# Projection stores from GpSimd's queue instead of SyncE's, in a hybrid attention and mLSTM encoder layer

## The chip, the cores and the metric

The kernel runs on one core of one Trainium2 chip. The metric is the device time of one execution in microseconds (us). The core has five engines, each of which works through its own queue of instructions in order: TensorE (PE in the profile; its weight loads are PEld), VectorE (DVE), ScalarE (ACT), GpSimd (POOL) and SyncE (SP). DMA transfers are issued by SyncE and by GpSimd, and carried out by 16 DMA engines that both share. In the profile the transfers of SyncE are queue q1 (hardware_dynamic), those of GpSimd queue q0 (software_dynamic).

## What is computed

One encoder layer over two sequences, a prompt of 1024 tokens and a sample of 2048, each with 16 learned meta tokens ahead of it and a model width of 1024:

```python
xn = _rmsnorm(h, g_pre)
proj = xn @ w_in + b_in
na_q, na_k, na_v, na_z, ml_qk, ml_v, ml_z, ml_o, ml_g, mg = jnp.split(proj, SPLIT_IDX, axis=-1)
ya = _neighbourhood_attention(na_q, na_k, na_v, na_rpb)
ya = (ya * jax.nn.silu(na_z)) @ w_a
yb = (_mlstm_branch(ml_qk, ml_v, ml_g, ml_o, ml_conv_w, ml_head_g) * jax.nn.silu(ml_z)) @ w_b
ga, gb = jnp.split(jax.nn.sigmoid(mg), 2, axis=-1)
y = (ga * ya + gb * yb) @ w_out
return h + _rmsnorm(y, g_post)
```

The input projection has 6672 columns. Neighbourhood attention has 8 heads of width 64 on a grid of rows of 64 tokens, with windows of 8 by 16; the mLSTM has 4 heads of width 128 and runs in both directions. All products are taken in float32, which the kernel makes from a high and a low part: three matmuls for one.

## The kernel before

**Two strands.** `run` weaves two generators into one order of TensorE's instructions. `dense` does the projections and, at the end, the merge and output products; `sparse` does the token mixers, in the order of `STEPS`: mLSTM of the prompt, attention of the prompt, mLSTM of the sample, attention of the sample. Each strand yields after some matmuls with their estimated cost, and `run` lets the other go on by as much. A strand of `sparse` starts when the columns that it needs are done. `PLAN` names the order of `dense`: which 1024 tokens, and which columns (m and v for mLSTM and values, n for attention, g for the merge gates), and then six final blocks of 512 tokens.

**Order within the queues.** TensorE's order is the order in which the program was written. The queues of the other engines, SyncE's and GpSimd's too, are ordered when the kernel is built (`schedule_with_timeline_sim=True`), by when a model of the chip takes an instruction to be ready. Two helpers tie this order: `held()` queues VectorE's and ScalarE's instructions behind those traced so far, and `behind()` (L205) queues what is traced in it behind `self.marks`, the last instruction that `mark(start)` saw on VectorE, ScalarE and SyncE. `mark` is called after each projection evacuation (in `fm_evac` and `tm_unit`) and after each piece of `sparse`. The loads of `tload` (L944), the stores of normalised inputs in `beside` (L562) and the side work on weights and inputs are traced inside `behind()`.

**Feature-major columns.** `fm_half` takes 128 columns of the projection as weights (a tile `whl` with their high and low parts, four copies, loaded in `wpump`, L304 and L310) and 512 tokens as the moving side, 24 matmuls in `mm3` (L218 to L220) into a PSUM bank `pj` of three. `fm_evac` brings the result into an SBUF tile `st` (four copies) with bias, activation and scale; the columns z take a second copy of `st`. Then the tile is stored to a tensor in device memory: MQ and MK for the mLSTM (L714, and L716 for the meta tokens), GT, NQ, NK, NZ and SZ for the rest (L723), and a small padded copy of the meta tokens' keys, NKM (L730). `sgates`, which does the attention and gate columns with seven half products for eight, ends in the same `fm_evac`; its matmuls are L988 to L990.

**Token-major columns.** `tm_unit` takes tokens as weights and 256 or 264 columns as the moving side (L787 to L789), for the values (NV, MV), the output gate (TO) and the mLSTM's gates (GA). Two blocks of 128 tokens are gathered in a tile `stT` (four copies) and `tm_store` writes them: GA at L825 and L827, TO at L830, MV at L834 and L836, the meta tokens' values NVM at L840, and NV at L846, four transfers a tile.

**Who reads what is stored.** The mLSTM loads MK and MQ (`raw`, L1433), MV (`va`, L1503), SZ and TO (L1634, L1635), its own keys again (`kf`, L1616) and rows of decay (`um`, L1622). The attention loads NQ, NK, NKM, NV, NVM and NZ (L1184 to L1220). The final blocks load GT (`tg`, L1892).

**What GpSimd does.** It issues the stores of NV (L846), the loads and stores of the side work (`wprep`: `pr` L587 and `po` L605; `nprep`: `xr` L619, L634, L635; `tprep`: `xr` L664, L678), the attention's masks (`kx`, L1200) and one-hot rows (`qB`, L1113), and it clears small tiles. All other transfers are issued by SyncE, among them the loads of the weights (`whl`, `wraw` L289), the stores of prepared weights (L341), the inputs (`xr` L408, `xt` L415) and the outputs.

Of the kernel before, what the change touches and what calls it, by code (L numbers as in the profile page):

```python
# [18 lines left out]
P = 128  # L19
# [3 lines left out]
NM = 16  # L23
# [115 lines left out]
class K:  # L139
# [542 lines left out]
    def fm_evac(self, col, s, t0, meta, chunks, ps):  # L682

        nc, wp = self.nc, self.wp
        bi = (col // P) if col < 4608 else 36 + (col - 4624) // P
        bias = self.bfm[:, bi:bi + 1]
        start = len(nc.cur_bb.bb.instructions)
        st = wp.tile([P, HALF], F32, name="st", bufs=4)
        m = NM if meta else 0
        n = 512 + m  # L690
        for (c0, c1), p in zip(chunks, ps):
            o, q = st[:, c0:c1], p[:, :c1 - c0]
            if s == 0 and col < C_GA:
                b = max(c0, m)
                if b > c0:
                    nc.vector.tensor_tensor(q[:, :b - c0], q[:, :b - c0], self.rm, op=ALU.mult)
                nc.vector.tensor_tensor(q[:, b - c0:], q[:, b - c0:], self.rr[:, t0 // 512, b - m:c1 - m], op=ALU.mult)
            if col < C_NK:
                nc.scalar.activation(o.rearrange("p (b r c) -> p r b c", r=8, b=4), q.rearrange("p (r b c) -> p r b c", r=8, b=4),
                                     AF.Identity, bias=self.bq8[:, bi:bi + 1], scale=0.125)  # L700
            elif C_NZ <= col < C_MQ or C_MZ <= col < C_MO:
                zb = wp.tile([P, HALF], F32, name="st", bufs=4)
                nc.scalar.activation(zb[:, c0:c1], q, AF.Identity, bias=bias)
                nc.scalar.activation(o, q, AF.Tanh, bias=self.bfh[:, bi:bi + 1], scale=0.5)
                nc.vector.scalar_tensor_tensor(o, o, 1.0, zb[:, c0:c1], op0=ALU.add, op1=ALU.mult)
            elif col >= C_GA:
                nc.scalar.activation(o, q, AF.Tanh, bias=self.bfh[:, bi:bi + 1], scale=0.5)
            else:
                nc.scalar.activation(o, q, AF.Identity, bias=bias)
        if C_MQ <= col < C_MV:  # L710
            dst = (self.MQ if col < C_MK else self.MK)
            h = (col % 512) // P
            lo = 0 if meta else NM + t0
            nc.sync.dma_start(dst[s][h][:, lo:lo + n], st[:, :n])  # L714
            if meta:
                nc.sync.dma_start(dst[1 - s][h][:, :NM], st[:, :NM])  # L716
            self.mark(start)
            return
        if col >= C_GA:
            dst = self.GT[s][(col - C_GA) // P]  # L720
        else:
            dst = (self.NQ, self.NK, None, self.NZ, None, None, None, self.SZ)[col // 512][s][(col % 512) // P]
        nc.sync.dma_start(dst[:, t0:t0 + 512], st[:, m:n])  # L723
        self.mark(start)
        if meta and C_NK <= col < C_NV:
            km = wp.tile([P, 64], F32, name="km", bufs=1)
            nc.gpsimd.memset(km, 0.0)
            nc.gpsimd.tensor_copy(km[:, 8:24], st[:, :NM])
            nc.gpsimd.tensor_copy(km[:, 40:56], st[:, :NM])
            nc.sync.dma_start(self.NKM[(col % 512) // P][:, :], km)  # L730

    def fm_half(self, col, w, x, s, t0, meta, done=None, tags=None, late=None):
        if not meta:
# [77 lines left out]
    def tm_store(self, col, wd, s, n, cnt, tok, st):  # L811
        nc, wp = self.nc, self.wp

        def rows(d, c0, c1, lo):
            return d[lo:lo + n * cnt, c0:c1].rearrange("(a p) c -> p a c", p=n)

        f = col % 512
        if col >= C_MO:
            c0 = col - C_MO
            no = min(wd, 512 - c0)  # L820
            if wd > no:
                g = wd - no
                if tok is None:
                    for q in range(2):
                        nc.sync.dma_start(self.GA[q][0:NM, :], st[:n, 0, no:wd])  # L825
                else:
                    nc.sync.dma_start(rows(self.GA[s], 0, g, NM + tok), st[:, :, no:wd])  # L827
            if tok is not None:
                nc.scalar.activation(st[:, :, :no], st[:, :, :no], AF.Tanh, scale=0.5)
                nc.sync.dma_start(rows(self.TO[s], c0, c0 + no, tok), st[:, :, :no])  # L830
        elif col >= C_MV:
            if tok is None:
                for q in range(2):
                    nc.sync.dma_start(self.MV[q][0:NM, f:f + wd], st[:n, 0, :wd])  # L834
            else:
                nc.sync.dma_start(rows(self.MV[s], f, f + wd, NM + tok), st[:, :, :wd])  # L836
        else:
            if tok is None:
                for lo in (8, 40):
                    nc.sync.dma_start(self.NVM[lo:lo + NM, f:f + wd], st[:n, 0, :wd])  # L840
            else:
                for a in range(cnt):
                    for r in range(2):
                        row = (tok + a * P) // 64 + r
                        dst = self.NV[s][:, row * 8:row * 8 + 8, f:f + wd]
                        nc.gpsimd.dma_start(dst, st[r * 64:r * 64 + 64, a, :wd])  # L846
# [1356 lines left out]
```

## Time and profile before

| what | value |
|---|---|
| median of 3 runs | 2685.29 us (2685.11 to 2685.42) |
| the profiled execution | 2684.88 us |
| its span, first to last instruction | 2682.8 us |
| mean granted clock of TensorE over the span | 0.996 |
| HBM read, written | 543.72 MB, 253.60 MB |

The profile is of one execution. Its lines name an engine, a line of the kernel and an operation, with "out<-in" for the tiles that it writes and reads. A wait stands as "who <- what released it", with the total in us, the number of waits and the longest. "SPq" and "POOLq" are the queues in which SyncE and GpSimd issue DMA transfers. A stretch of time stands as from:to, its length, the busy time of each engine with its number of instructions, the granted clock of TensorE (PEclk, 1.00 is full speed), the mean busy share of the 16 DMA engines and the rate in GB/s. Matmuls overlap, so the busy time of TensorE counts overlapping ones once.

### The profile page before, as it was taken

The page shows a single profiled execution, that of the slowest core. Times are in us where ns is not written, and L with a number is a line of the kernel's source. Part 1 is how long each engine was busy: PE and PEld are TensorE (multiplying, and loading weights), DVE is VectorE, ACT ScalarE, POOL GpSimd, SP SyncE. Part 2 cuts the span into 40 slices and gives each one's busy share as a digit, 9 for nine tenths or more (in the row PEclk, how much of TensorE's full clock was granted, in tenths as well). Part 3 has the DMA queues.
Part 4 walks back from the last instruction along what each step waited for, and adds up shares of the span by engine and source line. Part 5 has one row for each costly group of instructions (what it writes and reads, how often), then busy time and mean ns, then how long its engine had stood idle before and what let it go on. Part 6 is the DMA issues. An engine that isn't in the chain of part 4 may idle for free.

```text
span 2682.8 us, 47074 instructions
## 1 busy us (share of the span) xinstructions
PE 2640.1 (98%) x15928; PEld 2330.7 (87%) x15928; DVE 1940.1 (72%) x5262; ACT 1441.0 (54%) x3388; POOL 195.3 (7%) x418
## 2 busy tenths in 40 slices
PE   9999998999999999999999999999999999999998
PEld 7998897899978999888888888887889898989888
DVE  5655678788667878546686776867478989898954
ACT  5423555554445655546665666656366666656521
POOL 0111130011301115000000000000000000000000
PEclk9999999999999999999999999999999999999999
DMA  9899988799866998978889998899899999998975
GB/s 370 331 334 335 331 289 306 278 339 312 294 223 235 328 331 289 319 234 285 261 270 346 362 299 261 273 351 336 281 312 319 288 306 287 280 304 261 310 255 209
DMA packets 393520, 800.49 MB, mean 298 GB/s; under 512 B 50528, under 2 KB 173360, under 8 KB 389440
## 3 DMA queue, kind: packets, MB, share of 16 engines
q1 hardware_dynamic: 361728, 697.24, 77.9%
q0 software_dynamic: 31552, 100.25, 10.1%
q8 instruction: 126, 2.06, 0.3%
q14 instruction: 114, 0.93, 0.1%
HBM read 543.72 MB, written 253.60 MB: 297 GB/s over the span
## 4 chain that ended last, share of the span: by engine, by line
PE 89%; DVE 4%; DMA 4%; ACT 1%; issue 1%; SPq 0%; POOL 0%; DVEq 0%; ACTq 0%
PE pj L218 9%; PE pj L220 9%; PE pj L219 9%; PE pj L988 8%; PE pj L990 7%; PE pj L989 7%; PE pj L787 5%; PE pj L789 5%; PE pj L788 5%; PE pj L1950 3%; PE pj L1949 3%; PE pj L1951 3%; PE sm L1283 3%; PE tr L1268 2%; DMA whl<-w 1%
## 5 line engine op out<-in xcount | busy, mean ns | idle before, releaser
L218 PE MATMUL pj<-xh,whl 128*128 128x512 f32 (+1 forms) x960 | 369.5, 385 | 8.2 <-DMA whl<-w 6.2
L220 PE MATMUL pj<-xh,whl 128*128 128x512 f32 (+1 forms) x960 | 361.3, 376 | 0.0
L219 PE MATMUL pj<-xl,whl 128*128 128x512 f32 (+1 forms) x960 | 360.4, 375 | 0.2 <-DVE xl L446 0.2
L787 PE MATMUL pj<-whl,xh 128*128 128x256 f32 (+1 forms) x1152 | 330.7, 287 | 0.0
L789 PE MATMUL pj<-whl,xl 128*128 128x256 f32 (+1 forms) x1152 | 327.0, 284 | 0.0
L788 PE MATMUL pj<-whl,xh 128*128 128x256 f32 (+1 forms) x1152 | 326.7, 284 | 0.0
L787 PEld LDWEIGHTS pj<-whl,xh 128*128 128x128 f32 x1152 | 219.0, 190 | 0.4
L1949 PE MATMUL pj<-whl,mh 128*128 128x256 f32 x768 | 218.3, 284 | 0.9 <-DMA whl<-w 0.9
L788 PEld LDWEIGHTS pj<-whl,xh 128*128 128x128 f32 x1152 | 218.9, 190 | 0.2
L789 PEld LDWEIGHTS pj<-whl,xl 128*128 128x128 f32 x1152 | 218.8, 190 | 0.0
L218 PEld LDWEIGHTS pj<-xh,whl 128*128 128x128 f32 x960 | 181.2, 189 | 40.8 <-issue 5.3
L1950 PE MATMUL pj<-whl,mh 128*128 128x256 f32 x768 | 216.3, 282 | 0.0
L1951 PE MATMUL pj<-whl,mlo 128*128 128x256 f32 x768 | 215.5, 281 | 0.0
L220 PEld LDWEIGHTS pj<-xh,whl 128*128 128x128 f32 x960 | 181.3, 189 | 35.0
L219 PEld LDWEIGHTS pj<-xl,whl 128*128 128x128 f32 x960 | 181.6, 189 | 30.4 <-issue 1.0
L988 PE MATMUL pj<-xh,whl 128*128 128x512 f32 x512 | 206.7, 404 | 1.1 <-ACT pj L1005 1.1
L990 PE MATMUL pj<-xh,whl 128*128 128x512 f32 x512 | 202.0, 395 | 0.0
L989 PE MATMUL pj<-xl,whl 128*128 128x512 f32 x512 | 201.0, 393 | 0.0
L1275 DVE TENSOR_TENSOR pts<-tr,pts 96x384 fp32r<-96x384 f32 (+2 forms) x192 | 118.6, 617 | 57.2 <-ACT pts L1270 55.2
L1270 ACT ACTIVATE pts<-tr 96x384 fp32r<-96x384 f32 (+2 forms) x192 | 103.6, 539 | 100.8 <-PE tr L1268 100.1
L218 PE MATMUL pj<-yh,whl 128*128 128x512 f32 x384 | 154.1, 401 | 0.0
L219 PE MATMUL pj<-yl,whl 128*128 128x512 f32 x384 | 151.5, 394 | 0.7 <-DVE yl L1851 0.7
(380 smaller groups left out, 6866.1 us busy)
## 6 DMA issues: line engine op xcount, KB each, us to landing
whl<-w SPq DMA_DIRECT2D x131, 1024.0 KB
whl<-q SPq DMA_DIRECT2D x112, 512.0 KB
w<-whl SPq DMA_DIRECT2D x36, 1024.0 KB
wraw<-wu SPq DMA_DIRECT2D x48, 512.0 KB
gt<-st SPq DMA_DIRECT2D x96, 256.0 KB
tg<-gt SPq DMA_DIRECT2D x96, 256.0 KB
q<-po POOLq DMA_DIRECT2D x26, 512.0 KB, 6.7
xt<-xt SPq DMA_DIRECT2D x24, 512.0 KB
```

The costliest lines, as they stand in the source:

```text
L218: mm(out, ah, bh, start=start, stop=False)
L219: mm(out, ah, bl, start=False, stop=False)
L220: mm(out, al, bh, start=False, stop=stop)
L787: nc.tensor.matmul(o, xh, wh, start=k == 0, stop=False)
L788: nc.tensor.matmul(o, xh, wl, start=False, stop=False)
L789: nc.tensor.matmul(o, xl, wh, start=False, stop=k == KT - 1)
L988: mm(bank, w[:, 0, k], xh[:, k], start=fresh and k == 0, stop=False, skip_group_check=True)
L989: mm(bank, w[:, 0, k], xl[:, k], start=False, stop=False, skip_group_check=True)
L990: mm(bank, w[:, 1, k], xh[:, k], start=False, stop=k == 3, skip_group_check=True)
L1949: nc.tensor.matmul(o, mh[:, k, xs], wh, start=clear > 0 and k == 0, stop=False)
L1950: nc.tensor.matmul(o, mh[:, k, xs], wl, start=False, stop=False)
L1951: nc.tensor.matmul(o, ml[:, k, xs], wh, start=False, stop=clear < 2 and k == KT - 1)
```

## The change

Ten lines in `fm_evac` and `tm_store` issue their transfer from GpSimd's queue instead of SyncE's. Tensors, tiles, shapes and the order of the matmuls are the same. The stores of NV were issued by GpSimd already.

```diff
@@ fm_evac
-            nc.sync.dma_start(dst[s][h][:, lo:lo + n], st[:, :n])
+            nc.gpsimd.dma_start(dst[s][h][:, lo:lo + n], st[:, :n])
             if meta:
-                nc.sync.dma_start(dst[1 - s][h][:, :NM], st[:, :NM])
+                nc.gpsimd.dma_start(dst[1 - s][h][:, :NM], st[:, :NM])
...
-        nc.sync.dma_start(dst[:, t0:t0 + 512], st[:, m:n])
+        nc.gpsimd.dma_start(dst[:, t0:t0 + 512], st[:, m:n])
...
-            nc.sync.dma_start(self.NKM[(col % 512) // P][:, :], km)
+            nc.gpsimd.dma_start(self.NKM[(col % 512) // P][:, :], km)
@@ tm_store
-                        nc.sync.dma_start(self.GA[q][0:NM, :], st[:n, 0, no:wd])
+                        nc.gpsimd.dma_start(self.GA[q][0:NM, :], st[:n, 0, no:wd])
                 else:
-                    nc.sync.dma_start(rows(self.GA[s], 0, g, NM + tok), st[:, :, no:wd])
+                    nc.gpsimd.dma_start(rows(self.GA[s], 0, g, NM + tok), st[:, :, no:wd])
             if tok is not None:
                 nc.scalar.activation(st[:, :, :no], st[:, :, :no], AF.Tanh, scale=0.5)
-                nc.sync.dma_start(rows(self.TO[s], c0, c0 + no, tok), st[:, :, :no])
+                nc.gpsimd.dma_start(rows(self.TO[s], c0, c0 + no, tok), st[:, :, :no])
         elif col >= C_MV:
             if tok is None:
                 for q in range(2):
-                    nc.sync.dma_start(self.MV[q][0:NM, f:f + wd], st[:n, 0, :wd])
+                    nc.gpsimd.dma_start(self.MV[q][0:NM, f:f + wd], st[:n, 0, :wd])
             else:
-                nc.sync.dma_start(rows(self.MV[s], f, f + wd, NM + tok), st[:, :, :wd])
+                nc.gpsimd.dma_start(rows(self.MV[s], f, f + wd, NM + tok), st[:, :, :wd])
         else:
             if tok is None:
                 for lo in (8, 40):
-                    nc.sync.dma_start(self.NVM[lo:lo + NM, f:f + wd], st[:n, 0, :wd])
+                    nc.gpsimd.dma_start(self.NVM[lo:lo + NM, f:f + wd], st[:n, 0, :wd])
```

## The prediction

> **What bounds the kernel now.** I read the first page first: busy times, queues, and the chain that ended last.
>
> ```profile
> span 2682.8 us, 47074 instructions
> ...
> PE 2640.1 (98%) x15928; PEld 2330.7 (87%) x15928; DVE 1940.1 (72%) x5262; ACT 1441.0 (54%) x3388; POOL 195.3 (7%) x418
> ...
> q1 hardware_dynamic: 361728, 697.24, 77.9%
> q0 software_dynamic: 31552, 100.25, 10.1%
> ...
> PE 89%; DVE 4%; DMA 4%; ACT 1%; issue 1%; SPq 0%; POOL 0%; DVEq 0%; ACTq 0%
> ```
>
> TensorE is busy for 2640.1 of 2682.8 us and the chain runs along it. Its 15928 matmuls stay as they are, so what can be won or lost is its idle time (42.7 us) and what its clock loses. Beside it the DMA engines are nearly full: q1 (what SyncE issues) and q0 (what GpSimd issues) take 88% of them. Next I asked for TensorE's waits over the whole run (waiter, releaser, total us, times, longest), then for the stretches just behind the long ones (from:to, length, PE busy, granted clock, DMA share, GB/s).
>
> ```profile
> PE sm L220 <- DVE ktl L1574: 7.0, 6, 2.6
> PE pj L218 <- DMA whl<-w: 6.2, 2, 3.9
> ...
> PE sc L1699 <- ACT kh L1661: 2.8, 1, 2.8
> PE sm L218 <- ACT kth L1573: 1.9, 1, 1.9
> ...
> PE sc L1700 <- DVE kl L1662: 0.4, 1, 0.4
> ```
>
> ```profile
> 692.00:699.00 7.00, 6.99 (x35) 0.56 1.00 378
> 793.00:798.00 5.00, 4.53 (x13) 0.66 1.03 409
> 1817.00:1822.00 5.00, 4.64 (x20) 0.66 0.81 260
> ```
>
> The waits are few and short, but three of them (1.9 us before 691, 3.9 us before 793, 2.8 us before 1816) are followed by a stretch at a granted clock of 0.56 or 0.66, which costs another 7.0 x 0.44 = 3.1, 5.0 x 0.34 = 1.7 and 1.7 us. In all three a load was late, two of them behind ScalarE, whose own waits name them.
>
> ```profile
> ACT v L1679 <- DMA va<-mv: 8.8, 5, 3.8
> ...
> ACT kh L1661 <- DMA kf<-kf: 7.0, 4, 2.3
> ```
>
> `va` was the one before 691, `whl` before 793, `kf` before 1816. Those loads stand in SyncE's queue, and so do the stores that the change moves.
>
> **Why a load is late.** The chain of waits around 447 us shows a queue that takes only so many transfers at once: the load of `whl` was issued the moment that `wraw`, eight issues ahead of it and of no use to it, had landed (start, length, what).
>
> ```profile
> 447.26 9.31 DMA wraw<-wu
> ...
> 456.63 7.55 DMA whl<-w
> ```
>
> So a store in SyncE's queue can hold loads in two ways: it takes one of eight places until it has landed, and it keeps everything behind it waiting until its data is made. For the second way I read the waits of SyncE's queue.
>
> ```profile
> SPq L714 <- ACT st L709: 73.6, 26, 8.4
> ...
> SPq L723 <- DVE st L705: 48.6, 12, 7.1
> ```
>
> These two alone are 122.2 us in which SyncE stood at a projection store.
>
> **The change part by part.** *Count.* Rows of ten lines, of which these are the first, the longest and the last, add up to 322 moved stores (L714 48, L716 8, L723 192, L730 4, L825 2, L827 12, L830 24, L834 4, L836 24, L840 4); the columns are min/median/max ns.
>
> ```profile
> L714 SPq DMA_DIRECT2D mq<-st x24: 315/366/1227, 43.3 to 836.5; - x24
> ...
> L723 SPq DMA_DIRECT2D gt<-st x96: 319/374/2898, 1272.3 to 1990.7; - x96
> ...
> L840 SPq DMA_DIRECT2D nvm<-stT x4: 318/550/805, 362.7 to 395.7; - x4
> ```
>
> *Removed from SyncE:* 322 issues of about 0.37 us, 119 us, besides the waiting above. None of it lies on TensorE's path; it counts only where a load behind it is late.
>
> *Added to GpSimd:* 322 issues. Its nearest row is its own store of the same kind, L846; the dearest is L678.
>
> ```profile
> L846 POOL DMA_DIRECT2D nv<-stT x96 | 54.9, 575 | 81.7 <-DVE stT L805 25.4 <-DVE stT L803 21.0 <-DVE pts L1275 3.4
> ...
> L678 POOL DMA_DIRECT2D t01l<-xr x12 | 8.4, 697 | 5.1 <-DVE xr L641 3.4 <-DVE sm L1260 0.8 <-DVE yg L1298 0.8
> ```
>
> At 0.575 us that is 185 us (at 0.697, 224 us), so GpSimd goes from 195 to about 380 us of 2683: covered by its own idle time. I take it at nothing on the path. If the cover went, each issue would delay only the stores behind it.
>
> *Moved bytes.*
>
> ```profile
> gt<-st SPq DMA_DIRECT2D x96, 256.0 KB
> ```
>
> 288 of the stores carry about 256 KB, 75.5 MB, which leave q1 for q0. q1 takes 77.9% for 697.24 MB (0.112% a MB), q0 10.1% for 100.25 MB (0.101% a MB): 8.4% becomes 7.6%. Taken at nothing. What changes is the order: a store no longer stands ahead of a load in the same queue.
>
> *The store's own landing.* No row gives it on SyncE's side; GpSimd's rows (last number: us from issue to landing) bound it.
>
> ```profile
> q<-po POOLq DMA_DIRECT2D x26, 512.0 KB, 6.7
> ...
> nv<-stT POOLq DMA_DIRECT2D x96, 64.0 KB, 5.7
> ```
>
> So a 256 KB store should land in some 6 us (5.7 to 6.7). Before, a full queue took 7.6 and 9.3 us for its 1024 and 512 KB loads. The buffer `st` has four copies and a column needs 24 matmuls that start 0.24 us apart (the two rows below: start, length), 5.8 us; four copies are 23 us, and 12 us where a column takes two (z and sz). 6 us lie well inside, hence nothing.
>
> ```profile
> 788.68 0.39 PE L218 MATMUL pj<-xh,whl 128*128 128x512 f32 x1
> 788.92 0.40 PE L219 MATMUL pj<-xl,whl 128*128 128x512 f32 x1
> ```
>
> *What the stalls give back.* I price each late load by the part of SyncE's waiting in the 20 to 30 us ahead of it that was at a projection store. The three windows are 740 to 770, 672 to 692 and 1795 to 1818; of each stand the first and the last row and those of stores.
>
> ```profile
> SPq L714 <- ACT st L709: 24.4, 4, 6.9
> ...
> SPq L1634 <- DVE bs L1817: 0.3, 1, 0.3
> ```
>
> ```profile
> SPq L836 <- DVE kf L1530: 2.7, 1, 2.7
> ...
> SPq L1503 <- DVE cv L1649: 0.6, 1, 0.6
> ```
>
> ```profile
> SPq L1622 <- DMA xl<-xl: 2.2, 1, 2.2
> ...
> SPq L723 <- ACT cv L1442: 0.8, 1, 0.8
> ...
> SPq L723 <- DMA xh<-xh: 0.7, 1, 0.7
> ...
> SPq L723 <- ACT kh L1661: 0.4, 1, 0.4
> ```
>
> Stores are 24.4 of 29.0 us (5 rows), 2.7 of 14.4 (9 rows) and 1.9 of 13.9 (11 rows): 0.84, 0.19, 0.14. The stalls with their clock cost 3.9 + 1.7 = 5.6, 1.9 + 3.1 = 5.0 and 2.8 + 0.4 + 1.7 = 4.9 us. That gives 4.7 + 0.9 + 0.7 = 6.3 us. The other `whl` wait (2.3 us, at 464) I take at nothing, since the load ahead of it waited for the landing of `wraw`, not for a store; the `ktl` waits too (VectorE is full there).
>
> **Sum.** 2684.9 (the profiled execution: its span of 2682.8 and 2.1 around it; the median of the runs is 0.4 above) - 6.3 = **2678.6 us**. If all four late loads vanished with their clock, 5.6 + 5.0 + 4.9 + 2.3 = 17.8 less: 2667. If none moves: 2685.
>
> *A rule on the engine's port.* The slowest GpSimd issues above, 697 ns, lie beside VectorE work, 0.12 us over those of L846. The Trainium skill, "SBUF — State Buffer", section "SBUF: two separate sides", says that a DMA issued from GpSimd cannot get its descriptors written while VectorE runs an instruction that holds their shared port pair, and it advises SyncE or ScalarE as issuer: that speaks against this change. By its 3100 against 620 ns the 322 issues would take up to 800 us more of GpSimd, an estimate from that page; the trace shows nothing of that size.
>
> **The rivals.** *One: nothing moves (0.28).* The lateness is that of full DMA engines, not of the queue ahead.
>
> ```profile
> 760.00:765.00 5.00, 5.00 (x27) 1.00 0.30 105
> 790.00:795.00 5.00, 1.53 (x4) 0.88 1.03 409
> ```
>
> For it: at 790 the engines run at share 1.03 and 409 GB/s, and a load that is issued 3 us earlier lands no earlier there. Against it: at 760 they were at 0.30 while SyncE stood at `mk` stores. It gives 2685, within 2680 to 2690. The Trainium skill, "DMA: Bandwidth & Descriptors", section "Issuing engines are not separate DMA queues", holds with this rival: another issuer saves only the time to issue.
>
> *Two: GpSimd's order stops the projections (0.26, slower).* GpSimd too works its queue in order, and it stands long at side work (start, length, what, idle before it and its releaser).
>
> ```profile
> 824.51 0.72 POOL L678 DMA_DIRECT2D t01h<-xr  x1 [46.66 <-ACT xr L675]
> ```
>
> A projection store placed behind such an issue waits with it. From 23 us on, `st` is used up (12 us for z columns), ScalarE can't empty PSUM, and TensorE stops. At 46.7 us that is 24 us, plus the low clock, 2 to 3; a third of such an event, or one on a z column after a 20 us wait, is 8 to 10. Taken: 10, so 2695. Against it: during that wait SyncE did issue stores, so the build, which orders each queue by when it thinks work is ready, knew them as ready first. It decides where chip and plan differ by over 12 us. VectorE holding up GpSimd's issues would come out here too.
>
> *Three: the reordering itself (0.08).* 322 instructions change queue, SyncE's mark (what `behind()` queues loads after) is no longer set by these stores, and the build may lay out VectorE and ScalarE otherwise; the 7.0 us of `ktl` waits show what one such order costs. Half of it faster (2677), half slower (2692).
>
> **How the numbers follow.** Forecast 0.38, rivals 0.28, 0.26 and 0.08. What this kernel's measurement can tell from no change is about 0.2%, 5.4 us around 2685.3. Faster: 0.38 + 0.04 = 0.42; the same: 0.28; slower: 0.26 + 0.04 = 0.30. Both signs hold much, so the forecast's own range is 2667 to 2680; the range over the cases runs from 2666 to 2700, which leaves out full 24 us stops above and a gain on every wait below.
>
> **What would show it.** Right: the 3.9 us wait for `whl` near 789 and the low clock behind it are gone, SyncE's waits no longer name `st`, GpSimd is busy for 360 to 420 us, q1 shows about 622 MB. Rival one: these are so, and TensorE's waits are as long. Rival two: a long GpSimd wait at a `<-xr`, `q<-po` or `kx` issue, then ScalarE or VectorE waiting for a DMA of `st`, and TensorE for `pj`. Wrong in the root: TensorE's idle time changes by waits that hang on neither queue.

## The result, and the profile after

| | us |
|---|---|
| before, median of 12 runs | 2685.17 (2681.50 to 2686.68) |
| changed, median of 12 runs | 2691.36 (2688.38 to 2700.79) |
| ratio | 1.0029, 95% interval 1.0020 to 1.0037 |
| the profiled execution, changed | 2690.39, span 2688.6 |

The change makes the kernel slower: by 6.2 us by the medians, by 7.8 by the ratio (0.0029 x 2685; the interval is 5.4 to 9.9). First the lines of the changed kernel's first page that answer to those shown before.

```profile
span 2688.6 us, 47167 instructions
...
PE 2641.7 (98%) x15928; PEld 2331.0 (87%) x15928; DVE 1940.1 (72%) x5262; ACT 1441.5 (54%) x3388; POOL 381.8 (14%) x740
...
q1 hardware_dynamic: 308800, 621.13, 69.6%
q0 software_dynamic: 55680, 176.36, 17.4%
...
PE 82%; DMA 8%; DVE 4%; issue 4%; ACT 2%; POOL 0%; SPq 0%; DVEq 0%; POOLq 0%; ACTq 0%
```

Everything that was counted came out as counted: GpSimd is busy for 381.8 us (380 were forecast), q1 moves 621.13 MB (622). What was not counted is in the last line: transfers have 8% of the chain instead of 4%. TensorE's idle time is 2688.6 - 2641.7 = 46.9 us instead of 42.7. Its waits, whole run (waiter, releaser, total us, times, longest):

```profile
PE sm L218 <- ACT kth L1573: 5.2, 2, 4.8
...
PE sm L220 <- DVE ktl L1574: 4.7, 3, 2.1
PE pj L218 <- DMA whl<-w: 3.7, 2, 3.4
PE sm L1283 <- ACT prb L1251: 3.3, 5, 1.3
PE pj L218 <- DMA whl<-q: 3.0, 2, 2.7
...
PE sc L1699 <- ACT kh L1661: 2.4, 2, 1.3
```

The wait for `whl` near 789 is still there (3.4 us, it was 3.9); the one of 1.9 us before 691 has become 4.8; and a wait for `whl<-q`, 0.2 us before, is 3.0. The low clock follows these waits as it did, except that it is now at 1805 to 1810 instead of 1817 to 1822 (columns: from:to, length, PE busy, granted clock, DMA share, GB/s):

```profile
692.00:699.00 7.00, 6.80 (x37) 0.64 0.98 335
793.00:798.00 5.00, 5.00 (x15) 0.70 1.01 403
1805.00:1810.00 5.00, 4.68 (x16) 0.66 1.04 414
1817.00:1822.00 5.00, 3.78 (x16) 1.00 1.06 337
```

**Where the time goes.** TensorE's order is the same in all kernels here and all 15928 matmuls are in each trace, so I counted them through: the table gives how much later (+) or earlier (-) the same matmul starts than it did in the profile of before, at the matmuls that started there at 300 us and so on. One execution each: e1's and e4's traces are of the longest of their runs (6.3 and 4.7 us above the median), e5's of the shortest (5.0 below), the others within 1 us of theirs. The control e3, in which next to nothing moves, drifts by 5 us, so I rest on steps that recur at the same place in several kernels.

| kernel | 300 | 500 | 800 | 1000 | 1400 | 1500 | 1790 | 1850 | 2300 | 2680 |
|---|---|---|---|---|---|---|---|---|---|---|
| the change | +0.6 | -1.6 | -0.7 | -1.0 | -1.7 | +1.2 | +1.7 | +3.1 | +5.8 | +5.8 |
| e1: change, old order | -0.3 | -1.2 | -4.9 | +1.7 | +1.2 | +7.5 | +8.1 | +11.9 | +12.7 | +12.7 |
| e3: control, 8 small stores | +0.0 | -1.4 | -2.9 | -3.9 | -5.2 | -5.2 | -5.4 | -4.0 | -3.0 | -2.9 |
| e5: e1, loads pinned | -0.3 | +0.4 | -5.9 | -2.9 | -3.9 | -3.7 | -3.5 | -2.5 | -1.1 | -1.0 |
| e6: only the mark lost | +0.3 | +0.3 | +3.6 | +2.9 | +1.4 | +3.0 | +3.7 | +3.7 | +3.8 | +3.8 |
| e7: only gt moved | +1.5 | -0.8 | -0.3 | -0.3 | -1.6 | -1.0 | -1.2 | +3.0 | +4.4 | +4.4 |
| e8: loads moved, no store | -0.4 | +0.5 | -3.2 | -3.0 | -2.8 | -2.8 | -2.9 | -6.9 | -6.9 | -6.9 |
| e9: m stores, pinned | -0.1 | +2.1 | -4.4 | -0.9 | -1.7 | -1.7 | -1.8 | -3.4 | -2.8 | -2.0 |
| e12: m stores and loads | +0.2 | -1.5 | -4.3 | -4.3 | -4.3 | -4.3 | -4.4 | -8.4 | -7.7 | -7.6 |

Up to 1400 us the change is no slower. It loses 2.9 us between 1400 and 1500, 1.4 between 1790 and 1850 and 2.7 after 1850: in and behind the stretch of the gate columns (`gt`). One of these steps recurs. Between 1785 and 1815 the change, e1, e4, e5 and e7, which have the gt stores on GpSimd, lose 2.5 to 3.1 us; e3, e6 and e9, which have them on SyncE, between nothing and 0.3. e14, which has `va` and `kf` on GpSimd as well, wins 0.2.

### The profile page after: what moved, and what is told of

It is laid out like the page before. It is cut to its first block, busy times and chain, and to the rows that moved or that the text cites. A ratio compares the mean times of both kernels' runs of the same rounds, so it can differ in the third digit from the quotient of the medians.

```text
span 2688.6 us, 47167 instructions
## 1 busy us (share of the span) xinstructions
PE 2641.7 (98%) x15928; PEld 2331.0 (87%) x15928; DVE 1940.1 (72%) x5262; ACT 1441.5 (54%) x3388; POOL 381.8 (14%) x740
## 3 DMA queue, kind: packets, MB, share of 16 engines
q1 hardware_dynamic: 308800, 621.13, 69.6%
## 4 chain that ended last, share of the span: by engine, by line
PE 82%; DMA 8%; DVE 4%; issue 4%; ACT 2%; POOL 0%; SPq 0%; DVEq 0%; POOLq 0%; ACTq 0%
PE pj L218 9%; PE pj L220 9%; PE pj L219 9%; PE pj L988 7%; PE pj L990 6%; PE pj L989 6%; PE pj L787 5%; PE pj L789 5%; PE pj L788 5%; PE pj L1950 3%; PE pj L1949 3%; PE pj L1951 3%; PE sm L1283 2%; PE tr L1268 2%; DMA whl<-w 1%
```

## Theories and experiments

**A:** the build laid out VectorE's and ScalarE's queues in another order, and that order costs. **B:** the stores on GpSimd's queue cost in themselves. When A fell as the whole cause, B was split: **C**, SyncE's mark is no longer set by these stores, and loads are issued too early; **D**, stores in a queue of their own take their share of full DMA engines at once, and the loads land later. Ratios are to before, on the same chip; the interval's half width of about 0.0009 is 2.4 us.

**e1: the change with the old order of VectorE and ScalarE.** The order that these two engines had before is written down (ORDER) and imposed.

```diff
+        for a, b in zip(names, names[1:]):
+            tc.add_manual_dep(by[b], a, NoSync)   # VectorE, ScalarE: as before
```

> All ten stores on GpSimd as in the change, but VectorE and ScalarE work through their instructions in exactly the order that they had before the change; only SyncE's and GpSimd's queues differ from before. Theory A (the time comes from the new order of VectorE and ScalarE that the build laid out): the 6.2 us of loss go, 2685 us or a little less (2680 to 2686.5), and the 5.0 us wait of TensorE near 692 and the 1.9 us one near 332 are gone. Theory B (the stores on GpSimd's queue themselves cost: GpSimd's own loads stand behind them): still 2689 to 2693, and ScalarE still waits for a load of x_sample that GpSimd issues before 692. Were the forecast of -6.3 us hidden by the order, 2677 to 2681.

2691.03 us, ratio 1.0029 (1.0018 to 1.0040): the loss stays, so A is not the whole cause, unless the imposed order costs something by itself (e2). The waits did what A said: the one near 332 is gone, the one near 692 down to 0.9 us, and by 800 us this kernel is 4.9 us ahead (table). But it gives back 6.6 us between 800 and 1000, where the old order meets loads that land at other times, and 6.3 us between 1400 and 1500. The last is one load (chain of waits of e1 at 1452 to 1467: start, length, what):

```profile
1448.73 16.09 DMA kf<-kf
...
1464.85 0.42 ACT kh L1661
```

`kf` has 128 KB and takes 16.09 us to land; TensorE waits 4.1 us for `kh`.

**e2: the stores on SyncE, VectorE and ScalarE in the changed kernel's order.** The same edit, the other way round.

> All ten stores on SyncE as before, but VectorE and ScalarE work through their instructions in exactly the order that the changed kernel had. Theory A (order): 2689 to 2694 us, as the changed kernel. Theory B (GpSimd's queue): 2683 to 2687, as before. A value between would give the order's share of the 6.2 us.

2703.77 us, 1.0071 (1.0059 to 1.0083), beyond both theories. An order that was laid out for one set of queues costs 19.5 us (2703.77 - 2684.29, the median of before beside it) on another. So orders can't be priced by swapping them alone, and the 6.6 us that e1 lost between 800 and 1000 are no loss of the change (-0.7 and -1.0 in the table). For the same reason e1 can't rule A out; e7 is the kernel with a loss and nearly no new order.

**e3: a control.** Only the eight small stores of the meta tokens (L730, L840) move.

> Only the 8 small stores of the meta tokens (NKM and NVM) are moved to GpSimd; the 314 others stay on SyncE. These 8 move next to no bytes and end before 400 us, but the build lays out VectorE's order otherwise from there on. Theory A: the time moves by some us although nothing that matters was moved (2680 to 2692, not within 1 us of before), and TensorE's waits differ after 400 us. Theory B: within 1 us of before, 2684 to 2686.5.

2682.33 us, 0.9991 (0.9982 to 1.0000), 2.0 us under the median of before beside it: neither clearly apart from it nor within the 1 us of theory B. So a new plan of the build may be worth 2 us by itself, and a difference of that size is no evidence for a mechanism.

**e4: only the feature-major stores** (L714, L716, L723, L730).

> Only the feature-major stores (252 of 322) are moved to GpSimd, the token-major ones stay on SyncE. Theory A: the loss or gain is that of another order, anywhere from 2680 to 2695, and not the fm share of 6.2 us. Theory B: the loss goes with the number of stores on GpSimd, 252 of 322 of 6.2 us, 2689 to 2691.5.

2693.97 us, 1.0041 (1.0029 to 1.0053): all of the loss, or more. Near 1465 it has e1's wait again (2.2 us, before none), near 1810 that for `whl<-q` (2.0 us).

**e5: e1, with 56 loads and stores of SyncE pinned** behind the transfer that they stood behind before (L944, L562).

```diff
+    for x, y in PINS:                             # e1's edges stay
+        tc.add_manual_dep(by[x], y, NoSync)
```

> As the first experiment (all ten stores on GpSimd, VectorE's and ScalarE's order as before), and besides 56 of SyncE's transfers (the 24 loads of L944 and the 32 stores of L562, both traced inside behind()) are queued behind the transfer that they stood behind before the change. Theory C (the stores used to be SyncE's mark; without it the 1 MB loads of L944 are issued up to 47 us earlier, t2l at 1445 instead of 1492, ahead of the urgent kf): the 4.1 us wait for kh near 1465 and its slow clock go, about 6 us off 2691.0, 2684 to 2687. Theory D (stores in a queue of their own take their share of the full DMA engines at once, and the loads land later): still 2689 to 2692, and the waits for kh near 1465 and for whl near 1810 stay.

2688.54 us, 1.0011 (1.0002 to 1.0020). It ran on another chip than e1, so the ratios are to be set against each other: 4.8 us less than e1, with an uncertainty of some 3.8. Its trace, of the shortest of its runs, has no wait near 1465; the one for `whl<-q` near 1800 stays (2.8 us), as theory D said. What the pins hold back is this (before, the change, e5; one transfer: ns, start):

```profile
L944 SPq DMA_DIRECT2D t2l<-t2l x1: 320/320/320, 1492.2 to 1492.2; - x1
```

```profile
L944 SPq DMA_DIRECT2D t2l<-t2l x1: 558/558/558, 1445.2 to 1445.2; - x1
```

```profile
L944 SPq DMA_DIRECT2D t2l<-t2l x1: 1126/1126/1126, 1484.6 to 1484.6; - x1
```

In the change this 1 MB load is issued 47 us earlier, and SyncE's queue shows what stands right behind it:

```profile
1445.18 0.56 SPq L944 DMA_DIRECT2D t2l<-t2l  x1
1445.83 0.58 SPq L1616 DMA_DIRECT2D kf<-kf  x1
```

The urgent `kf`. `tload` traces its loads inside `behind()`, and what held them back on SyncE was the mark that the projections' stores left there. With the pins, 1400 to 1500 us costs 0.2 us instead of e1's 6.3 (its shortest run against e1's longest).

**e6: all stores on SyncE, the mark alone taken away.**

```diff
-    def mark(self, start):
+    def mark(self, start, sp=True):
...
-            if x.engine in (DVE, Activation, SP):
+            if x.engine in (DVE, Activation) or sp and x.engine == SP:
...
-        self.mark(start)            # L717, L724, L808
+        self.mark(start, sp=False)
```

> All stores on SyncE as before; only mark() no longer records SyncE after the three places that store projections. Theory C: the loads of L944 move forward and the time goes up by as much as in the change, 2688 to 2692, with a wait for kh near 1460. Theory D: 2683 to 2687, as before, since the stores still stand in one queue with the loads.

2689.24 us, 1.0011 (1.0002 to 1.0020): slower without one store moved, with `t2l` at 1448.2. But it loses only 1.6 us between 1400 and 1500, and the wait for `kh` near 1460 that C expected is not there. It loses 3.3 between 500 and 800, by a wait near 691 that the change has too (4.8 us):

```profile
PE sm L218 <- ACT kth L1573: 6.0, 1, 6.0
```

In both kernels `kth` stands there behind `xsq` (L365) on ScalarE. With the mark gone the build has laid out VectorE and ScalarE anew (some 300 of 5262 and 180 of 3388 instructions stand elsewhere than before). So losing the mark costs, but here more by a new order, which is A, than by early loads; for C itself speaks e5 beside e1, which share their order. Neither explains all: no wait for `whl<-q` near 1800 is here (0.3 us).

**e7: only the 96 stores of the gate columns move.**

```diff
-        nc.sync.dma_start(dst[:, t0:t0 + 512], st[:, m:n])
+        (nc.gpsimd if col >= C_GA else nc.sync).dma_start(dst[:, t0:t0 + 512], st[:, m:n])
```

> Only the 96 stores of the gate columns (gt) are moved to GpSimd, the 226 others stay on SyncE. Theory D, and C too: the waits for kh near 1460 and for whl near 1805 are there although hardly anything was moved before 1270 us, 4 to 8 us slower than before, 2688 to 2693. By D the gt stores land in about 7 us while the loads beside them take 11 to 16. If the loss came from the stores of the m columns, 2684 to 2686.

2688.84 us, 1.0013 (1.0004 to 1.0022). Here `t2l` keeps its place (1492.1), and the stretch from 1400 to 1500 costs 0.6 us: so the wait near 1460, which I expected by either theory, is not there. Of the 56 transfers behind the mark none starts over 8 us earlier or later than before, and of VectorE's and ScalarE's instructions only 16 and 12 stand elsewhere: neither C nor, but for these, A is in this kernel. The step at 1790 to 1850 is there, 4.2 us, with the wait for `whl<-q`:

```profile
PE pj L218 <- DMA whl<-q: 2.2, 2, 1.9
```

What lies behind it is in the change too. First the queues of before from 1778 to 1805 (packets, MB, share of 16 engines), then those of the change from 1778 to 1806:

```profile
q1 hardware_dynamic: 4660, 10.75, 104.2%
```

```profile
q1 hardware_dynamic: 4160, 9.47, 91.9%
q0 software_dynamic: 400, 1.31, 11.8%
...
gt<-st POOLq DMA_DIRECT2D x5, 256.0 KB, 6.8
```

The engines are full in both. Before, all of them worked for the loads and the few stores among them; now the stores take 11.8%, and q1 moves 9.47 MB in 28 us (0.338 a us) instead of 10.75 in 27 (0.398). The stores land in 6.8 us (the last column); the weight load that TensorE waits for, twice as large, needs 12.63:

```profile
1793.14 12.63 DMA whl<-q
```

Like beside like, from each transfer's issue to its last completion mark in the trace, between 1778 and 1806: the 256 KB gt stores landed in 9.6 to 9.9 us from SyncE's queue before, and in 5.8 to 7.8 from GpSimd's in the change. The 512 KB `whl<-q` loads, on SyncE in both, took 9.4 to 10.9 before, 10.9 to 14.3 in the change and 11.1 to 13.4 in e7. That is theory D. It shows only where the engines are full: the median of all 96 gt stores is 6.0 us in both kernels.

And who waits has changed sides. ScalarE's waits from 1785 to 1806, before and in the change:

```profile
ACT st L707 <- DMA gt<-st: 3.1, 1, 3.1
...
ACT kh L1661 <- DMA kf<-kf: 1.9, 1, 1.9
```

```profile
ACT kh L1661 <- DMA kf<-kf: 6.1, 2, 4.9
```

Before, the store was late, and four copies of `st` stood for it; now `kf` is late, and behind it is TensorE. The Trainium skill, "DMA: Bandwidth & Descriptors", section "Queues, rings and completion order", says that each DMA engine takes turns between the queues that have work for it, a packet at a time. The landing times agree with it. The Trainium skill, "DMA: Bandwidth & Descriptors", section "Issuing engines are not separate DMA queues", which the prediction drew on, says that another issuer saves only the time to issue; the same stores landing in 5.8 to 7.8 us instead of 9.6 to 9.9 speak against reading it that way.

**e8: D turned round.** All stores on SyncE; the mLSTM's loads `va` and `kf` go to GpSimd.

```diff
-        nc.sync.dma_start(va[:np_, :nch, 0:P],
+        nc.gpsimd.dma_start(va[:np_, :nch, 0:P],
...
-                nc.sync.dma_start(kf, self.KF[s][h][:, t0:t0 + BL])
+                nc.gpsimd.dma_start(kf, self.KF[s][h][:, t0:t0 + BL])
```

> All stores stay on SyncE; instead the mLSTM's small urgent loads va (L1503) and kf (L1616), 128 KB each, are issued by GpSimd. Theory D turned round: in a queue of their own they land in about 7 us instead of 9 to 16, the waits for va near 691 and for kf near 1816 go, with their slow clock up to 9.9 us: 2675 to 2681. If a transfer's queue makes no difference to when it lands: 2683 to 2688, and the landing times of va and kf stay at 9 us and more.

2678.54 us, 0.9981 (0.9969 to 0.9993): faster, by 3.7 us between 500 and 800 and 4.0 between 1790 and 1850 (table), the two places where it was expected; the second step is 4.0 in e10 and e12 too. Landing times (last column) and TensorE's wait for `kh`, which was 2.8 us:

```profile
va<-mv POOLq DMA_DIRECT2D x96, 128.0 KB, 5.8
```

```profile
kf<-kf POOLq DMA_DIRECT2D x48, 128.0 KB, 5.6
```

```profile
PE sc L1699 <- ACT kh L1661: 1.1, 1, 1.1
```

From SyncE's queue before, `kf` had a median of 6.6 us; its slowest tenth took 10.0 or more, here 7.0 or more. So the second queue helps the late ones most. It is not only a matter of places in SyncE's queue: e7 took 96 transfers out of it and lost, e8 took 152 out of it and won. But places help as well. The `whl<-q` load that TensorE waits for in the change is issued at 1783.3 here (before 1790.9) and needs 12.1 us, almost as in the change, and TensorE doesn't wait for it.

**e9: only the m and token-major stores move** (126 of 322; the 118 of the expectation leave out the eight of L716), with e1's order and e5's pins.

> Only the stores of the m columns and the token-major ones (mq, mk, mv, to, gg, nvm; 118 of 322) are moved to GpSimd; those of gt, nq, nk, nz and sz stay on SyncE. VectorE's and ScalarE's order and the place of the 56 loads behind the mark are kept as before. If the forecast's gain is real and was only eaten later by the gate columns' stores (theory D), what was won by 800 us in the fifth experiment (5.9 us) is kept: 2679 to 2682 us. If those stores cost as well, 2685 to 2689.

2683.59 us, 0.9994 (0.9985 to 1.0003): no difference that shows, and not the 2679 to 2682 expected. In its trace the gain by 800 us is there (4.4 us), and 3.5 of it goes between 800 and 1000, where I put it down to VectorE's imposed order (`sm L1236 <- DVE sm L1260`, 3.2 us instead of 1.5).

**e10: `raw` (L1433) and `um` (L1622) go to GpSimd as well as `va` and `kf`.**

> All stores on SyncE; va, kf (L1616), raw (L1433) and um (L1622), all the mLSTM's loads for one block, are issued by GpSimd. By theory D each lands in about 6 us in that queue: as good as va and kf alone or better, 2674 to 2680. Against: GpSimd's queue is worked in order, raw waits for a buffer, and kf behind it may be late: then 2683 to 2690.

2688.12 us, 1.0014 (1.0004 to 1.0025): the second answer. GpSimd works in order and now stands at `raw` too, and in the same stretch, 1195 to 1222, TensorE stands at the start of the sample's mLSTM; that the one makes the other is argued, not shown:

```profile
POOL raw L1433 <- DVE g_e L1334: 9.4, 1, 9.4
...
PE sm L1343 <- issue: 6.1, 1, 6.1
```

**e11: the weights `whl` (L304, L310) go to GpSimd.**

> All stores on SyncE; the weights whl (L304 and L310, 379 transfers) are issued by GpSimd. By theory D they land sooner beside SyncE's loads and the waits for whl (6.2 us before) shrink, while the loads left on SyncE (va, kf) land later: 2678 to 2688. If a queue of its own gives no share, 2684 to 2687 with the waits for whl unchanged.

2709.43 us, 1.0091 (1.0077 to 1.0105), far above what was expected. No wait for `whl` is among TensorE's long ones any more, but GpSimd now stands waiting for weight buffers to come free, 430.2 us at one line for one releaser alone, with everything else that it does behind it:

```profile
POOL whl L304 <- PE pj L990: 430.2, 81, 7.1
```

**e12: the m and token-major stores, and `va` and `kf`, on GpSimd;** the stores of gt, nq, nk, nz and sz stay on SyncE, no order imposed.

> The stores of the m columns and the token-major ones, and the loads va and kf, are issued by GpSimd; the stores of gt, nq, nk, nz and sz stay on SyncE; no order is kept by hand. If the two gains add (5 us by 800 us from the stores, 4 near 1811 from kf), 2673 to 2678. If the new order of VectorE, or the lost mark, takes them back, 2680 to 2688.

2677.62 us, 0.9974 (0.9963 to 0.9985): 7.0 us faster than before by the ratio, 13.7 faster than the change by the medians, the lowest median here. Whether its stores add to e8 isn't told: the intervals of the two overlap widely.

**e13: the gt stores on ScalarE's queue.**

> Only the 96 gt stores are moved, this time to ScalarE's queue instead of GpSimd's. What was open: are the loads beside them late because the stores are issued at once instead of behind the loads (then any other issuer does it), or only because GpSimd's queue gets a share of its own? The first: the wait for whl near 1800 is there (about 2 us and a slow clock), 2687 to 2691. The second: no such wait, 2683 to 2687. Beside it ScalarE has 96 issues more, some 36 us at SyncE's 0.37 us each, which its 46% of idle time should cover.

2700.32 us, 1.0056 (1.0043 to 1.0070), outside both ranges, and it answers its question in part. Between 1778 and 1806 the gt stores land in 6.7 to 7.1 us, as from GpSimd, yet the `whl<-q` loads beside them in 9.0 to 11.2, as before, and TensorE has no wait for `whl<-q`. So stores that land soon don't by themselves make the loads late, as far as one trace with three stores there can say. But ScalarE's transfers shared SyncE's eight places, so that no more were under way than before; whether GpSimd's queue gets a share of its own, or only adds transfers under way, isn't told. The time went elsewhere: ScalarE's own issues had to wait for SyncE's transfers (1785 to 1816), and ScalarE is what `kh` needs:

```profile
ACT st L707 <- DMA whl<-q: 8.5, 1, 8.5
```

**e14: the whole change, with `va` and `kf` on GpSimd too.**

> The whole change, and besides va and kf (L1616) issued by GpSimd. If what the gt stores cost is only that va and kf land later, this gives it back: 2680 to 2685. If whl near 1800 and the early loads of L944 stay late, some of the loss stays: 2685 to 2691.

2692.67 us, 1.0028 (1.0018 to 1.0039): nothing given back. `kh` waits 1.1 us as in e8, but the weights are late as in the change (`whl<-q` 2.7 us), and near 332 it waits 2.2 us for `vwh`, as the change does (1.8).

## Why the prediction was wrong

2678.6 us and faster were forecast; it is 2691.36 and slower. Step by step:

*The count, GpSimd's share and the stores' own landing* were right: 96 gt issues take 541 ns each (575 taken), and they land in 6.0 us (5.7 to 6.7 estimated; first the group with its idle time, then the landing).

```profile
L723 POOL DMA_DIRECT2D gt<-st x96 | 51.9, 541 | 478.0 <-ACT st L707 380.5 <-ACT st L1599 21.0 <-ACT hb L1756 17.3
```

```profile
gt<-st POOLq DMA_DIRECT2D x96, 256.0 KB, 6.0
```

VectorE is busy for 72% of the span beside them. The Trainium skill, "SBUF — State Buffer", section "SBUF: two separate sides", says that GpSimd can't write the descriptors while VectorE holds the port pair that they share; a mean of 541 ns shows none of that, so leaving it out of the sum was right.

*Rival two* (GpSimd's order stops the projections, 0.26) ended on the right side for a reason that isn't there. Among the 200 largest groups of waits of the change none of ScalarE or VectorE is for a store of `st`; before there were these two, and one of VectorE (L318, 4.3 us for `mq<-st`):

```profile
ACT st L703 <- DMA mq<-st: 6.5, 1, 6.5
...
ACT st L707 <- DMA gt<-st: 3.1, 1, 3.1
```

*"Moved bytes. Taken at nothing. What changes is the order: a store no longer stands ahead of a load in the same queue"* is the step that failed. The stores also stood *behind* loads. In full DMA engines SyncE's one queue made who came later wait, and the stores could afford it: 9.6 to 9.9 us to land before, 5.8 to 7.8 in a queue of their own, while the loads that TensorE needs went from 9.4 to 10.9 up to 10.9 to 14.3. e7 puts a price of 3.4 us on it (2688.84 - 2685.40), with an interval from 1 to 6. I had looked for what a store does to the load behind it, and not for what the load ahead did to the store.

*The mark* stood in rival three, with 0.08 for all reordering and half of that as a gain. Losing it costs 3.8 us in e6 (2689.24 - 2685.40; interval 0.5 to 5.4), mostly by the new order near 691, and some 4.8 with e1's order (e1 against e5). It could have been read in the code: `behind()` on SyncE's side hung on just the instructions that left SyncE.

*What the stalls give back*, 4.7 + 0.9 = 5.6 us up to 800: three kernels with the old order (e1, e5, e9) are ahead by 4.9, 5.9 and 4.4 us there, but that the sum agrees is luck. Near 691 (670 to 700), where 0.9 was forecast, they win 2.2, 5.4 and 5.0 us, and e8, whose stores are all on SyncE, 5.4 too. Near 789 (780 to 800), where 4.7 was forecast, they win 1.4, 2.5 and 1.6. The control e3 is 2.9 us ahead by 800. The wait for `whl` near 789 was to vanish and still has 2.5 to 3.0 us in e1 and e5; the window from 740 to 770, in which SyncE stood at stores for 24.4 of 29.0 us, shows why. In the change SyncE's waits in it are these:

```profile
SPq L1634 <- DVE bs L1817: 17.0, 1, 17.0
SPq L408 <- DVE nwt L166: 7.5, 1, 7.5
SPq L408 <- DVE num L1738: 6.7, 1, 6.7
```

With the stores gone, SyncE stands as long at the loads that came behind them, since their buffers weren't free. The first `whl` load after it is issued at 770.6 in both kernels. A wait at a store is no price of the store; it is one only if what stands behind it is ready. In the change itself little is left of this gain (0.7 us by 800), because the build's new order put `kth` behind `xsq` (L365) on ScalarE near 691, among others: the 4.8 us above, which is 0.9 in e1 and gone in e5.

*The 0.7 us near 1816* came (the wait for `kh` fell from 2.8 to 1.1), and was outweighed by the wait for `whl<-q` some 10 us earlier.

The parts measured alone, the mark 3.8, the gate columns 3.4 and the m and token-major columns -1.9 (e9, with the old order), make 5.3 us of the 6.2, with an uncertainty of some 2.4 us each; the 100 stores of nq, nk, nz, sz and nkm were not measured alone. So the agreement is not a proof. Open stays what the gt stores do to the attention after 1850 us (2.7 us in the change, 1.4 in e7; VectorE waits 2.6 us for a load of `tg` near 2009, before 1.0), and whether the loads are late because a second queue gets its own share or because more transfers are under way at once.

## What to carry to other kernels

Where the DMA engines are full, a queue of its own lets a transfer land sooner, and the others later: give the second queue to the small loads that something waits for (e8, e12), and leave stores with slack behind the loads. Before pricing a wait in a queue, look whether what stands behind the waiting instruction is ready; and before moving instructions to another engine, look what else hangs on where they were (marks, orders, what the build plans), since here that cost about as much (e6, 3.8 us) as the queue itself (e7, 3.4 us). A planned order is fitted to its queues: a control that moves next to nothing (e3) says how much of a difference may be the plan.

## What the runs showed of the hardware

- Two queues beside each other, in some 28 us with full engines: the same 256 KB stores landed in 9.6 to 9.9 us from SyncE's queue (before) and in 5.8 to 7.8 from GpSimd's (the change), while SyncE's 512 KB loads went from 9.4 to 10.9 up to 10.9 to 14.3. Over the whole run the slow ones differ more than the medians: 128 KB `kf` loads had a median of 6.6 us from SyncE (before) and 5.6 from GpSimd (e8), and the slowest tenth took over 10.0 and over 7.0.
- In these builds SyncE and ScalarE share eight places for transfers under way: in e13 ScalarE stood 8.5 us at a store until a load that SyncE had issued was in.
- In the change GpSimd issued 740 - 418 = 322 transfers more, and its busy time rose by 186.5 us, 0.58 us each, with VectorE busy for 72% of the span.
